# A hybrid decoder trunk on one core: one plain gate/up pair fewer in three FFNs, with the fourth of the seven products ahead of the third and the weights rounded four items ahead

## The chip, the core and the metric

The kernel runs on one core of one Trainium2 chip. The engines have short names in the profile: PE is TensorE (matmuls; PEld is its weight load), DVE is VectorE, ACT is ScalarE, POOL is GpSimd and SP is SyncE, which here only issues DMAs. Each engine takes its instructions in its own fixed order, and they wait for each other by semaphores. The metric is the device time of one execution in microseconds; of several runs the median counts.

## The reference

Two layers, each with an FFN, a mixer (a gated linear recurrence and a sliding-window attention side by side) and a second FFN, every one between two RMSNorms. Sequence 512, model width 1024, hidden width 2816 (22 tiles of 128), all float32. The change lies in the FFNs:

```python
def swiglu(h, w_gate, w_up, w_down):
    return (jax.nn.silu(h @ w_gate) * (h @ w_up)) @ w_down

for l in range(DEPTH):
    h = rms_norm(x, gn[0])
    x = x + 0.5 * rms_norm(swiglu(h, w_ffn1_gate[l], w_ffn1_up[l], w_ffn1_down[l]), gn[1])
    ...
    h = rms_norm(x, gn[4])
    x = x + 0.5 * rms_norm(swiglu(h, w_ffn2_gate[l], w_ffn2_up[l], w_ffn2_down[l]), gn[5])
```

## The kernel before

**Matmuls in float32 by three passes.** Each operand is split into a high half, rounded to a format that TensorE takes at full speed, and a low half, the remainder. A product is hi x hi + hi x lo + lo x hi, three matmuls (`mm3`, line 381). For weights the halves are called `whi` and `wlo`; `wlo` is first used by the third matmul of a group. Rounding is done while the kernel runs: ScalarE casts (L325), and the remainder comes either from VectorE (a subtraction, L332) or, for some items, from a negation on ScalarE (L329) and a DMA of GpSimd's queue that adds the raw weight onto it (L330).

**The stream of weights.** `Stream` (line 156) holds the order in which the weights are used as a list of items, each one tile of 128 x 1024 or less. Raw tiles (`w32`, four buffers) are loaded by SP's DMAs (L241, L244); rounded ones have six buffers (`WS`). `ahead` (line 342) rounds items until `most` = `AHEAD` = 3 items past the current one are done, as long as fewer than six are in use.

**An FFN's first half** is 22 pairs of a gate tile and an up tile, `gated(...)` or `fast(...)`. In the first FFN of layer 0 the first seven pairs are plain; in the other three FFNs the first `PLAIN` = 4 are: two in one opening group (`quad`), the others one by one, each two products `project` of 8 x 3 matmuls of 512 columns. During them VectorE and ScalarE prepare sums of the activations (`pre.sums()`, L564, L459 to L466, L401, L402): four are needed, two are issued after the opening group and one ahead of each single pair.

**The other pairs are fast blocks** (`sevenths`, line 851): gate and up together are a 2 x 2 block product done with seven products instead of eight, each 4 x 3 matmuls of 256 columns. A block uses four weight items: a (products 1 and 2; negation and DMA), b (5 and 7; the sums L312 and L313 are rounded, remainder by VectorE), c (6 and 4; sums L318 and L319, remainder by VectorE) and d (product 3; half a tile, negation and DMA). VectorE puts the products together in L875, L877, L882 and L883, ScalarE copies the first product (L865) and applies the silu in place (L895), and VectorE multiplies (L896). While block k runs, the weights of later blocks are rounded.

**The second half** is the down product (`down`, line 637), which starts with four plain weight items and goes on with a seven-product scheme of its own over rows, whose items are quarters (`quarter`, line 255; casts L282, remainders L287). Its first operands are the first four results of the FFN, split by L401 (ScalarE) and L402 (VectorE); the last fast block issues that split after its second product (`early`, line 887).

**What sets the order.** TensorE's order is that of the program text (with some coroutines put in by a clock of the planner's own). The other engines' instructions are ordered by the framework's scheduler; those marked `pin` keep the text's order among themselves. So the text's order on TensorE is exact, and on VectorE, ScalarE and the DMA queues a small edit can move instructions.

Of the kernel before, what the change touches and what calls it, by code (L numbers as in the profile page):

```python
# [33 lines left out]
    head=2600.0, level=5000.0, last=3400.0, chunks=2600.0, blocks=350.0, norm=2370.0, gate=8000.0,  # L34
    values=1200.0, scores=2000.0, exp=9000.0, shares=4500.0, turn=1900.0, turned=3000.0, rest=1200.0, lent=4200.0, apart=4000.0, block=2000.0, pair=4000.0, att0=1260.0, att1=12300.0,
)
W32, WS, AHEAD, TAIL, PLAIN, FIRST, EARLY, LATE = 4, 6, 3, 4, 4, 7, 4, 8
TURN = 0
LEAD = 8
ORDER = ("p1", "p6", "p2", "p7", "p5", "p4", "p3")  # L40
# [5 lines left out]
def trunk(ctx: ExitStack, tc: tile.TileContext, xin, wall, gains, lbT, hgain, sinks, c_dist, c_mask, c_ident, out):  # L46
# [12 lines left out]
    def nm(s):  # L59
        seq[0] += 1  # L60
        return f"{s}_{seq[0]}"

    def big(dt=F32, shape=None):
        return sb.tile(shape or [P, S], dt, tag="s", name=nm("s"), bufs=SLOTS)
# [4 lines left out]
    def acc():  # L69
        return ps.tile([P, S], F32, tag="acc", name=nm("acc"), bufs=5)  # L70

    def aux():
        return ps.tile([P, S], F32, tag="aux", name=nm("aux"), bufs=3)
# [82 lines left out]
    class Stream:  # L156
# [27 lines left out]
        def gates(self):  # L184
# [6 lines left out]
            self.plain(1)  # L191

        def rows(self, kt, fast):


# [183 lines left out]
    ws = Stream()  # L379
# [7 lines left out]
    def wmm(o, b, mv, start, stop, poll=True):  # L387

        mm3(o, b[2:], mv, start, stop)
        ws.used(b)  # L390
        if poll:
            order.poll()
# [217 lines left out]
    class Late(Quarters):  # L610
# [23 lines left out]
        def raw(self, half, i):  # L634
            return [cut(self.src[self.k0 + 4 + k], HALF[half]) for k in range(4)] if i else self.x1

    def down(src, kt, l, n, nxt, fast):


# [176 lines left out]
    def quad(pre, halves):  # L816

        o = [acc() for _ in range(4)]
        blocks = {}
        ws.pinned = halves  # L820
        for half in (0, 1) if halves else (None,):
            c = WHOLE if half is None else HALF[half]
            for k in range(KT):
                order.until(lambda: pre.have[half or 0] > k)
                for j in range(4):
                    if (k, j) not in blocks:
                        blocks[k, j] = ws.next(uses=2 if halves else 1)
                    wmm(o[j][:, c], blocks[k, j], cut(pre.h[k], c), k == 0, k == KT - 1)
            ws.pinned = False
        return o  # L830

    def project(pre, get=acc):
        o = get()
        for k in range(KT):
            wmm(o, ws.next(), pre.h[k], k == 0, k == KT - 1)
        return o
# [12 lines left out]
    H2 = S // 2  # L849

    def sevenths(pre, between=lambda: None):

        def product(o, it, c, n):
            x = pre.operand(n)
            for k in range(4):
                wmm(o, ws.block(it, c + k), x[k], k == 0, k == 3)

        p1, p26, p57, p43 = acc()[:, :H2], acc(), acc(), aux()  # L860
        s, v = big()[:, :H2], big(F32, [P, 2, H2])
        m = sb.tile([P, 4, H2], F32, tag="m", name=nm("m"), bufs=1)
        w = ws.whole()
        product(p1, w, 0, 1)
        nc.scalar.copy(s, p1)  # L865
        product(p26[:, :H2], w, 4, 2)
        between()
        w = ws.whole()
        product(p57[:, :H2], w, 0, 5)
        product(p57[:, H2:], w, 4, 7)  # L870
        c = ws.whole()
        product(p26[:, H2:], c, 0, 6)
        pairs = [p.rearrange("p (i t) -> p i t", i=2) for p in (p26, p57, p43)]

        nc.vector.tensor_tensor(m[:, 0:4:2, :], pairs[0], s.unsqueeze(1).to_broadcast([P, 2, H2]), op=ALU.add)  # L875

        nc.vector.tensor_tensor(v, pairs[1], m[:, 2:3, :].to_broadcast([P, 2, H2]), op=ALU.add)  # L877
        w = ws.whole()
        product(p43[:, H2:], w, 4, 3)
        product(p43[:, :H2], c, 4, 4)  # L880

        nc.vector.tensor_tensor(m[:, 3, :], p57[:, :H2], v[:, 1, :], op=ALU.add)  # L882
        nc.vector.tensor_tensor(m[:, 1:3, :], pairs[2], v[:, ::-1, :], op=ALU.add)  # L883
        return m

    def fast(pre, a, start):
        def early():
            if j == FT - 1:
                for i in range(EARLY):
                    a[i] = split(a[i])  # L890

        for j in range(start, FT):
            m = sevenths(pre, early)
            z = big(F32, [P, 2, H2])
            nc.scalar.activation(out=m[:, 0:2, :], in_=m[:, 0:2, :], func=AF.Silu)  # L895
            nc.vector.scalar_tensor_tensor(z, m[:, 0:2, :], -1.0, m[:, 2:4, :], op0=ALU.mult, op1=ALU.mult)  # L896
            a.append(z.rearrange("p i t -> p (i t)"))

    def ffn(l, n, pre, nxt, halves=True):
        a = []  # L900

        def gated(og, ou):
            z, u = big(), big()
            if first:
                pin(nc.vector.tensor_tensor(z, og, pre.rb, op=ALU.mult))
                nc.scalar.activation(out=z, in_=z, func=AF.Silu)
                nc.vector.tensor_tensor(u, ou, pre.rb, op=ALU.mult)
                nc.vector.tensor_tensor(u, u, z, op=ALU.mult)
            else:
                nc.scalar.activation(out=z, in_=og, func=AF.Silu)  # L910
                pin(nc.vector.tensor_tensor(u, ou, z, op=ALU.mult))
            a.append(u)

        first = isinstance(pre, First)
        o = quad(pre, halves)
        if first:
            o.append(project(pre))
            o.append(project(pre, aux))
            order.until(lambda: pre.rb is not None)
        if not first:  # L920
            pre.sums()
            pre.sums()
        for j in range(2):
            gated(o[2 * j], o[2 * j + 1])
        if first:
            gated(o[4], o[5])
            for j in range(3, FIRST):
                if j > 3:
                    order.until(lambda: pre.laid)
                    pre.sums()  # L930
                if j == 4:
                    pre.sums()
                gated(project(pre), project(pre))
            fast(pre, a, FIRST)
        else:
            for j in range(2, PLAIN):
                pre.sums()
                gated(project(pre), project(pre))
            fast(pre, a, PLAIN)
        return down(a, FT, l, n + 1, nxt, True)  # L940
# [129 lines left out]
    def mixer(l, pre, nxt):  # L1070
# [177 lines left out]
        def branches(get):  # L1248

            v = sevenths(pre)  # L1250
            src = get()
            for i in range(2):
                g = big(F32, [P, 2, H2])
                nc.scalar.activation(out=g, in_=v[:, 2 * i : 2 * i + 2, :], func=AF.Tanh, scale=-0.5 if i else 0.5)
                p = acc()
                for k in range(4):
                    wmm(p, ws.next(), src[k], k == 0, k == 3)
                g = g.rearrange("p i t -> p (i t)")
                nc.vector.scalar_tensor_tensor(g, g, 1.0, p, op0=ALU.add, op1=ALU.mult)
                yield g  # L1260
# [36 lines left out]
    pre = First()  # L1297
# [69 lines left out]
    for l in range(DEPTH):  # L1367
        pre = ffn(l, 0, pre, (l, 2), halves=l > 0)
        pre = mixer(l, pre, (l, 4))
        pre = ffn(l, 4, pre, (l + 1, 0) if l + 1 < DEPTH else None)  # L1370
# [81 lines left out]
```

## Time and profile before

| | us |
|---|---|
| three runs | 2100.14, 2100.54, 2103.34 |
| median | 2100.54 |
| the profiled execution | 2100.66 |
| its span, first to last instruction | 2098.9 |

The profile is of one execution. Its page gives each engine's busy time; the chain of waits goes back from the last instruction to what released each step; the timeline lists instructions with their start, their length and, in brackets, the idle time of the engine before them and what ended it. A row marked x2 stands for two instructions in a row. Starts of two neighbouring rows are the better measure of pace, since the lengths overlap a little. TensorE's granted clock is 0.999 of full speed over the span.

| engine | busy, us | share of the span |
|---|---|---|
| TensorE, matmuls | 2090.3 | 100% |
| VectorE | 1550.5 | 74% |
| ScalarE | 1122.4 | 53% |
| GpSimd | 154.2 | 7% |

### The profile page before, as it was taken

What the parts mean: (1) busy time and instruction counts of PE and PEld (TensorE: products, weight loads), DVE (VectorE), ACT (ScalarE), POOL (GpSimd) and SP (SyncE); (2) the same over time, 40 slices, a digit from 0 to 9 for tenths busy, and PEclk for the clock granted to TensorE, in tenths of its full rate; (3) what the DMA queues carried; (4) which work ended last, traced back from release to release, by engine and by line L of the source; (5) the groups of instructions that cost most, each with busy time, mean ns of one, the idle gap of its engine ahead of it and who ended that gap; (6) DMA issues with size and microseconds to landing.
All of it is one profiled execution on the core that took longest, in us unless ns stands there. A gap on an engine that the chain in (4) does not pass through costs nothing.

```text
span 2098.9 us, 35207 instructions
## 1 busy us (share of the span) xinstructions
PE 2090.3 (100%) x13549; PEld 1875.3 (89%) x13549; DVE 1550.5 (74%) x2705; ACT 1122.4 (53%) x1899; POOL 154.2 (7%) x188
## 2 busy tenths in 40 slices
PE   9999999999999999999999999999999999999998
PEld 8899988887888999998899998898778989999987
DVE  5877886766776777789587778767687758777884
ACT  6555564456454555556455556554653545555562
POOL 0011000000000011110001110000000000111000
PEclk9999999999999999999999999999999999999999
DMA  8577653312236357774447775632122563677651
GB/s 246 152 181 184 178 157 135 111 61 71 71 101 203 127 122 182 181 198 122 154 114 176 183 181 150 191 120 92 51 81 61 136 193 103 159 182 181 184 160 51
DMA packets 148071, 298.35 MB, mean 142 GB/s; under 512 B 16992, under 2 KB 74816, under 8 KB 147904
## 3 DMA queue, kind: packets, MB, share of 16 engines
q1 hardware_dynamic: 122416, 228.16, 33.2%
q0 software_dynamic: 25344, 67.91, 18.7%
q8 instruction: 106, 1.74, 0.3%
q14 instruction: 61, 0.50, 0.1%
q10 hardware_dynamic: 144, 0.05, 0.0%
HBM read 213.43 MB, written 14.73 MB: 109 GB/s over the span
## 4 chain that ended last, share of the span: by engine, by line
PE 88%; DMA 0%; DVE 0%; ACT 0%; SPq 0%; issue 0%; ACTq 0%
PE acc L115 64%; PE aux L115 22%; PE aux L125 1%; PE acc L125 1%; DMA wlo<-w 0%; DMA w<-wall 0%; SPq L241 0%; DVE s L402 0%; ACT whi L282 0%; DVE s L731 0%; ACT s L600 0%; DVE s L712 0%; DVE s L896 0%; DVE wlo L287 0%; ACT m L895 0%
## 5 line engine op out<-in xcount | busy, mean ns | idle before, releaser
L115 PE MATMUL acc<-s,whi 128*128 128x256 f32 (+1 forms) x4952 | 1059.3, 311 | 0.4 <-ACT whi L325 0.3
L115 PEld LDWEIGHTS acc<-s,whi 128*128 128x128 f32 x4952 | 808.0, 191 | 51.3 <-issue 3.2
L115 PE MATMUL acc<-s,wlo 128*128 128x256 f32 (+1 forms) x2476 | 766.6, 310 | 0.1
L115 PEld LDWEIGHTS acc<-s,wlo 128*128 128x128 f32 x2476 | 472.6, 191 | 25.0 <-DVE wlo L332 0.4
L325 ACT CAST whi<-w 128x1024 fp32r<-128x1024 f32 (+1 forms) x341 | 316.6, 948 | 237.6 <-PE acc L115 95.5
L115 PE MATMUL acc<-whi,s 128*128 128x512 f32 x1264 | 413.6, 393 | 0.1
L325 ACT CAST whi<-tt 128x1024 fp32r<-128x1024 f32 x154 | 161.4, 1048 | 326.5 <-DVE tt L319 184.2
L332 DVE TENSOR_TENSOR wlo<-w,whi 128x1024 fp32r<-128x1024 f32 (+1 forms) x181 | 218.3, 1215 | 151.4 <-ACT whi L325 149.6
L115 PEld LDWEIGHTS acc<-whi,s 128*128 128x128 f32 x1264 | 237.1, 188 | 54.7 <-ACT whi L325 1.6
L332 DVE TENSOR_TENSOR wlo<-tt,whi 128x1024 fp32r<-128x1024 f32 x154 | 188.1, 1221 | 98.8 <-ACT whi L325 98.7
L115 PE MATMUL acc<-wlo,s 128*128 128x512 f32 x632 | 246.4, 390 | 0.0
L115 PE MATMUL aux<-s,whi 128*128 128x256 f32 (+1 forms) x1248 | 230.4, 285 | 0.0
L330 POOL DMA_DIRECT2D wlo<-w x160 | 137.8, 863 | 1258.6 <-ACT wlo L329 704.9
L115 PE MATMUL aux<-whi,s 128*128 128x512 f32 x592 | 196.7, 390 | 0.0
L115 PEld LDWEIGHTS aux<-s,whi 128*128 128x128 f32 x1248 | 195.2, 192 | 1.1 <-issue 0.5
L115 PE MATMUL aux<-s,wlo 128*128 128x256 f32 (+1 forms) x624 | 177.5, 284 | 0.0
L115 PEld LDWEIGHTS acc<-wlo,s 128*128 128x128 f32 x632 | 118.7, 188 | 23.4
L115 PEld LDWEIGHTS aux<-whi,s 128*128 128x128 f32 x592 | 111.1, 188 | 22.8
L329 ACT ACTIVATE wlo<-w 128x1024 fp32r<-128x1024 f32 (+1 forms) x160 | 129.8, 844 | 0.0
L401 ACT CAST s<-s 128x512 fp32r<-128x512 f32 (+1 forms) x164 | 88.4, 580 | 71.5 <-DVE s L460 67.9
L115 PEld LDWEIGHTS aux<-s,wlo 128*128 128x128 f32 x624 | 119.8, 192 | 0.3
L115 PE MATMUL aux<-wlo,s 128*128 128x512 f32 x296 | 115.2, 389 | 0.0
(186 smaller groups left out, 2128.6 us busy)
## 6 DMA issues: line engine op xcount, KB each, us to landing
w<-wall SPq DMA_DIRECT2D x267, 512.0 KB, 3.7
wlo<-w POOLq DMA_DIRECT2D x83, 512.0 KB, 5.5
w<-wall SPq DMA_DIRECT2D x288, 128.0 KB, 3.3
wlo<-w POOLq DMA_DIRECT2D x77, 256.0 KB, 3.3
x_d<-s SPq DMA_DIRECT2D x48, 256.0 KB, 2.1
s<-x_d SPq DMA_DIRECT2D x48, 256.0 KB, 5.5
w<-wall SPq DMA_DIRECT2D x34, 256.0 KB, 3.0
s<-wall SPq DMA_DIRECT2D x64, 128.0 KB, 3.6
```

The source lines that it names most:

```text
L115: nc.tensor.matmul(o, lhsT, rhs, start=start, stop=stop)
L125: nc.tensor.transpose(o, src, ident)
L325: i = nc.scalar.copy(it.hi[:, c], w[:, c])
L329: nc.scalar.mul(it.lo[:, c], w[:, c], -1.0)
L330: nc.gpsimd.dma_start(it.lo[:, c].bitcast(F32), w[:, c], accum_op=ALU.add)
L332: nc.vector.tensor_tensor(it.lo[:, c], w[:, c], it.hi[:, c].bitcast(F32), op=ALU.subtract)
L401: nc.scalar.copy(hi, src)
```

## The change

Three edits. `PLAIN` goes from 4 to 3: in three of the four FFNs one pair that was plain becomes a fast block, and the two sums that were issued one each ahead of two single pairs are both issued ahead of the one that is left. Inside a fast block, and in the mixer's gate blocks, which call the same function, product 4 is issued ahead of product 3, so item c is used up before d is taken. And while an FFN's fast blocks run, `most` is 4 instead of 3. Line numbers after 877 shift: what was L882 and L883 is L881 and L882, L895 and L896 keep theirs.

```diff
-W32, WS, AHEAD, TAIL, PLAIN, FIRST, EARLY, LATE = 4, 6, 3, 4, 4, 7, 4, 8
+W32, WS, AHEAD, TAIL, PLAIN, FIRST, EARLY, LATE = 4, 6, 3, 4, 3, 7, 4, 8
...
-        w = ws.whole()
-        product(p43[:, H2:], w, 4, 3)
         product(p43[:, :H2], c, 4, 4)
+        product(p43[:, H2:], ws.whole(), 4, 3)
...
+        ws.most = AHEAD + 1
         for j in range(start, FT):
             m = sevenths(pre, early)
...
+        ws.most = AHEAD
...
             for j in range(2, PLAIN):
-                pre.sums()
+                for _ in range(2 // (PLAIN - 2)):
+                    pre.sums()
                 gated(project(pre), project(pre))
```

The scheduler answers with other orders on VectorE and ScalarE. The first place is one lap of VectorE in the fast blocks of the second FFN, before the change (`tt` are the summed weights: L312 and L313 make b's, L318 and L319 c's; `m` is the block's result):

```order
L312 TENSOR_TENSOR tt_8716<-w_1524_8517,w_1525_8519 128x512
L313 TENSOR_TENSOR tt_8716<-w_1525_8519 128x512
L332 TENSOR_TENSOR wlo_8715<-tt_8716,whi_8714 128x1024
L318 TENSOR_TENSOR tt_8747<-tt_8716,w_1525_8519 128x512
L319 TENSOR_TENSOR tt_8747<-tt_8747,w_1524_8517 128x512
L875 TENSOR_TENSOR m_8680<-acc_8675,s_8678 128x2x256
L877 TENSOR_TENSOR s_8679<-acc_8676,m_8680 128x512
L332 TENSOR_TENSOR wlo_8746<-tt_8747,whi_8745 128x1024
L882 TENSOR_TENSOR m_8680<-acc_8676,s_8679 128x256
L883 TENSOR_TENSOR m_8680<-aux_8677,s_8679 128x512
L896 TENSOR_SCALAR s_8798<-m_8680 128x512
```

The same lap after the change:

```order
L875 TENSOR_TENSOR m_8619<-acc_8614,s_8617 128x2x256
L877 TENSOR_TENSOR s_8618<-acc_8615,m_8619 128x512
L332 TENSOR_TENSOR wlo_8624<-tt_8625,whi_8623 128x1024
L318 TENSOR_TENSOR tt_8657<-tt_8625,w_1515_8439 128x512
L881 TENSOR_TENSOR m_8619<-acc_8615,s_8618 128x256
L319 TENSOR_TENSOR tt_8657<-tt_8657,w_1514_8437 128x512
L882 TENSOR_TENSOR m_8619<-aux_8616,s_8618 128x512
L332 TENSOR_TENSOR wlo_8656<-tt_8657,whi_8655 128x1024
L896 TENSOR_SCALAR s_8737<-m_8619 128x512
L312 TENSOR_TENSOR tt_8752<-w_1534_8564,w_1535_8566 128x512
L313 TENSOR_TENSOR tt_8752<-w_1535_8566 128x512
```

b's remainder and c's sums, which stood ahead of L875, now stand behind L877, and c's remainder behind L882. ScalarE's order in that lap is the copy, the casts of b and c, then the rounding of d and of the next a, then the silu, before and after; of d and a it takes the two casts first before the change, and d's cast and negation first after it. The lap of the first FFN keeps the old order on both engines.

The second place is ScalarE at the end of the fast blocks of the second FFN, before the change (L895 is the silu of the last block but one, L865 the copy of the last block's first product, L325 the cast of a plain item of the down product, L282 casts of its quarters, L401 those of its first operands):

```order
L895 ACTIVATE m_9956<-m_9956 128x512
L865 COPY s_10087<-acc_10083 128x256
L401 COPY s_10124<-s_7733 128x512
L325 COPY whi_10200<-w_1764_10047 128x1024
L401 COPY s_10128<-s_7737 128x512
L401 COPY s_10132<-s_7821 128x512
L325 COPY whi_10223<-w_1765_10052 128x1024
L401 COPY s_10136<-s_7909 128x512
L282 COPY whi_10281<-w_1776_10097 128x512 x2
L282 COPY whi_10332<-w_1787_10147 128x512 x2
```

After the change:

```order
L895 ACTIVATE m_10022<-m_10022 128x512
L325 COPY whi_10163<-w_1755_9966 128x1024
L325 COPY whi_10237<-w_1774_10094 128x1024
L325 COPY whi_10270<-w_1775_10099 128x1024
L282 COPY whi_10305<-w_1778_10134 128x512 x2
L282 COPY whi_10393<-w_1789_10167 128x512 x2
L865 COPY s_10157<-acc_10153 128x256
L401 COPY s_10218<-s_7733 128x512
L401 COPY s_10222<-s_7737 128x512
```

The copy and the first operands' casts, which stood ahead of the quarters, now stand behind all four of their casts. VectorE's remainders follow in the same way (L287, L875, L402), and the first FFN ends in the same new order.

## The prediction, on record before the changed kernel ran

> **What bounds the kernel now.** I read the page first, then the chain of waits, and only then the timelines of VectorE and ScalarE inside one fast block.
>
> ```profile
> span 2098.9 us, 35207 instructions
> PE 2090.3 (100%) x13549; PEld 1875.3 (89%) x13549; DVE 1550.5 (74%) x2705; ACT 1122.4 (53%) x1899; POOL 154.2 (7%) x188
> ```
> ```profile
> 717.69 43.37 PE acc L115 x276
> 761.06 2.88 PE aux L115 x24
> ```
>
> TensorE is busy for the whole span. The chain gives its pace: 24 matmuls of 256 columns, the two last products of a fast block, take 2.88 us, 0.120 each; a block has 84, 10.08 us. The 276 matmuls from 717.69 are 120 of the opening group of the FFN, two plain pairs of 48 and the first 60 of a block; 43.37 - 180 x 0.120 leaves 21.77 for the two pairs, 10.88 each. So the kernel is bound by TensorE, and something else decides whether it stays so: how late the rounded weights come. Here is one fast block on VectorE, late in the second FFN (start, length, instruction, idle time before it and what ended it), and then ScalarE's rows around it.
>
> ```profile
> 903.64 0.68 DVE L875 TENSOR_TENSOR m<-acc,s 128x512 f32<-128x512 f32 x1
> 904.36 0.69 DVE L877 TENSOR_TENSOR s<-acc,m 128x512 f32<-128x512 f32 x1
> 904.97 1.22 DVE L332 TENSOR_TENSOR wlo<-tt,whi 128x1024 fp32r<-128x1024 f32 x1
> 906.10 0.42 DVE L882 TENSOR_TENSOR m<-acc,s 128x256 f32<-128x256 f32 x1
> 906.43 0.68 DVE L883 TENSOR_TENSOR m<-aux,s 128x512 f32<-128x512 f32 x1
> 908.36 0.69 DVE L896 SCALAR_TENSOR_TENSOR s<-m 128x512 f32<-128x512 f32 x1 [1.25 <-ACT m L895]
> 908.97 0.68 DVE L312 TENSOR_TENSOR tt<-w,w 128x512 f32<-128x512 f32 x1
> 909.57 0.68 DVE L313 TENSOR_TENSOR tt<-w 128x512 f32<-128x512 f32 x1
> 911.37 1.22 DVE L332 TENSOR_TENSOR wlo<-tt,whi 128x1024 fp32r<-128x1024 f32 x1 [1.11 <-ACT whi L325]
> 912.51 0.68 DVE L318 TENSOR_TENSOR tt<-tt,w 128x512 f32<-128x512 f32 x1
> 913.23 0.69 DVE L319 TENSOR_TENSOR tt<-tt,w 128x512 f32<-128x512 f32 x1
> 913.84 0.68 DVE L875 TENSOR_TENSOR m<-acc,s 128x512 f32<-128x512 f32 x1
> ```
> ```profile
> 907.72 0.62 ACT L895 ACTIVATE m<-m 128x512 f32<-128x512 f32 x1
> 910.29 1.05 ACT L325 CAST whi<-tt 128x1024 fp32r<-128x1024 f32 x1 [1.70 <-DVE tt L313]
> 914.01 1.05 ACT L325 CAST whi<-tt 128x1024 fp32r<-128x1024 f32 x1 [2.67 <-DVE tt L319]
> 914.97 1.56 ACT L325 CAST whi<-w 128x512 fp32r<-128x512 f32 x2
> 917.91 0.62 ACT L895 ACTIVATE m<-m 128x512 f32<-128x512 f32 x1
> ```
>
> VectorE repeats after 913.84 - 903.64 = 10.20 us, longer than TensorE's 10.08, and no wait in that lap is for TensorE. It is a ring through both engines. From one silu (L895) to the next: product L896 0.64, L312 0.61, L313 0.60, cast of item b 0.72, its remainder (L332) 1.08, L318 1.14, L319 0.72, cast of c 0.78, first cast after it 0.96, then the two casts and two negations of d and the next a 2.94 up to the silu: 10.19. The busy shares (74%, 53%) hide this. TensorE loses nothing because 18 laps of 0.12 us eat only 2 us of the lead.
>
> **The change, part by part.** *Fewer plain pairs.* Three times 10.88 becomes 10.08: -2.4 us, all on TensorE's path.
>
> *The ring in these three FFNs.* By the order of the changed program, VectorE now takes b's remainder and L318, L319 after L875 and L877; c's cast waits for L319, and the silu still stands behind d's and a's rounding on ScalarE. The new lap, by the same rows: silu to L896 0.64, to L312 0.61, to L313 0.60, to L875 0.60 (as L312 to L313), to L877 0.72, to b's remainder 0.61, to L318 1.14, to the next independent one 0.60, to L319 0.33 (as L882 to L883), to c's cast 0.78, 0.96, then 2.94: 10.53 us. That is 0.45 over TensorE's 10.08, with no TensorE wait in it. Is there a lead to pay from? The last of a lap's results is the low half of the a-weights for the block after next:
>
> ```profile
> 771.99 0.61 ACT L325 CAST whi<-w 128x512 fp32r<-128x512 f32 x1
> 772.51 0.63 ACT L329 ACTIVATE wlo<-w 128x512 fp32r<-128x512 f32 x1
> 773.98 1.05 ACT L329 ACTIVATE wlo<-w 128x1024 fp32r<-128x1024 f32 x1
> ```
> ```profile
> 775.33 0.86 POOL L330 DMA_DIRECT2D wlo<-w  x1 [1.03 <-ACT wlo L329]
> ```
> ```profile
> wlo<-w POOLq DMA_DIRECT2D x83, 512.0 KB, 5.5
> wlo<-w POOLq DMA_DIRECT2D x77, 256.0 KB, 3.3
> ```
>
> L875 to c's cast is 4.18 (0.72 to 0.78 in that lap), then 0.96 + 2.94 to the silu; a's negation ends 0.1 later, POOL's DMA starts 0.30 after it (775.03 to 775.33) and lands 5.5 later: 14.0 us after L875. L875 can run 7.2 us into a block (60 matmuls), and the block after next needs that half at its third matmul, 20.16 + 0.24 - 7.2 = 13.2 us after L875. So the lead is already 0.8 short, and the ring's 0.45 goes to TensorE in every block.
>
> The first blocks. VectorE prepares four sums ahead of the fast blocks:
>
> ```profile
> 735.30 1.28 DVE L564 TENSOR_TENSOR s<-s,s 128x512 f32<-128x512 f32 x2
> 739.61 0.68 DVE L312 TENSOR_TENSOR tt<-w,w 128x512 f32<-128x512 f32 x1
> ```
>
> One sum takes 4.31 us here. Before, a whole plain pair hid the last; now the first block starts at 743.0 instead of 753.9 (761.06 less 60 x 0.120, and less 10.88). If the third sum still starts at 735.3, the fourth ends at 743.9; L318, L319 and c's cast follow at 745.4, a's negation ends 2.94 + 0.96 + 0.1 later at 749.4 and its DMA lands at 755.2. It is due at 743.0 + 10.08 + 0.24 = 753.3: 1.9 us of stall. So an FFN loses 1.9 at its second block, 0.8 at the fourth, then 15 x 0.45 = 6.8: 9.5, and three FFNs 28.5. Bounds: a landing 1 us shorter saves the 0.8 and 1.0 of the 1.9 (23 in all); one half a microsecond longer makes the way over the DMA (two blocks in 8.5 + 6.0 - 0.24 + 7.2 = 21.5) slower than the ring, 0.65 a block (36).
>
> *The end of the fast blocks, in all four FFNs.* With four items ahead, ScalarE has the rounding of the first quarter items (L282, four casts) ahead of the copy L865 of the last block and ahead of the L401 casts that make the first operands of the down product; before, the four L401 stood ahead of L282. This is how it goes now in the first FFN:
>
> ```profile
> 233.56 4.57 DMA wlo<-w
> ...
> 244.72 0.63 ACT whi L282
> ...
> 245.37 0.69 DVE wlo L287
> ```
> ```profile
> 240.94 0.40 PE L115 MATMUL acc<-whi,s 128*128 128x512 f32 x1
> ```
>
> The raw quarters land late, since one of their buffers waits for the last d accumulation (233.56 to 238.13); the last L282 starts at 244.72, 3.8 us after the down product has begun at 240.94. In the new order L865 follows at +0.52, L401 at +0.78, and on VectorE L287 at 245.37, L875 0.6 later and the low half (L402, 0.69) 0.6 after that: 247.3. TensorE needs it at its third matmul, 240.94 + 0.45. Stall 5.9 us. In the other three FFNs the last d comes with the longer ring:
>
> ```profile
> 927.55 0.86 POOL L330 DMA_DIRECT2D wlo<-w  x1 [8.39 <-DVE m L883]
> ```
> ```profile
> 938.40 0.62 ACT L282 CAST whi<-w 128x512 fp32r<-128x512 f32 x1 [0.59 <-DMA w<-wall]
> ```
>
> The last L282 starts 10.85 after that DMA. Now d's DMA starts 4.18 + 0.96 + 1.15 + 0.30 = 6.6 after L875, so the last L282 starts 17.4 after it and the low half is there at 20.0, while the down product is due 13.2 after L875 and at its third matmul 13.6. Stall 6.4; three FFNs 19.2. Bounds: if the quarters came early, L282 would still wait for the buffers of the last block, freed at its end: two casts, L865, L401 and L402 are then 2.7 us each (11 in all); the extra transfer that now stands ahead of the quarters in SP's queue makes 7 each (28).
>
> *TensorE's clock.* Five to six idle microseconds are new to it. The end of the program shows what thin use does (stretch, busy times, then the granted clock):
>
> ```profile
> 2088.00:2090.00 2.00, 2.00 (x15) 1.79 (x13) 0.69 (x1) 0.59 (x1) 0.00 (x0) 1.00 0.00 0
> 2090.00:2092.00 2.00, 0.38 (x2) 0.00 (x0) 1.38 (x2) 0.82 (x3) 0.00 (x0) 1.00 0.81 251
> 2094.00:2096.00 2.00, 0.86 (x4) 0.45 (x4) 0.62 (x1) 0.59 (x1) 0.00 (x0) 0.56 0.19 60
> ```
>
> Dense work ends at 2090, and a mean of 0.56 over 2094 to 2096 is half speed from about 2094.2 on. I take it that each of the four stalls does this and that the way back is as long: 4.2 us at half speed lose 2.1, four times 8.4. No row shows the way back; the bounds are nothing, and the first 24 matmuls of the down product at half speed, 5.4 each (22). [...]
>
> *Product four ahead of three.* Both end the block together; TensorE's count and L883's wait stay. It gives d 12 matmuls, 1.44 us, more. In the first block d's accumulation starts at about 747.8 (c's cast 745.4, then 0.96 + 1.15 + 0.30) and lands 3.3 later at 751.1; its first use of the low half is now due at 743.0 + 8.64 + 0.24 = 751.9, in the old place at 750.4, which would have been a stall of 0.7. In later blocks it has more than 1 us to spare. So I cost it at nothing. In the gate blocks of the mixer the order of VectorE and ScalarE is unchanged: nothing. In the first FFN the lap is the old one, 10.20: nothing.
>
> **The sum.** -2.4 + 28.5 + 5.9 + 19.2 + 8.4 = +59.6. The profiled execution took 2100.66 us (span 2098.9 and 1.8 around it), 0.1 over the median of 2100.54; so 2100.7 + 59.6 = 2160.3.
>
> **The rivals.** (1) The clock does not fall, as the two matmuls that can run in each stall may be enough: 2152. For it: in 2090 to 2092 it still stood at 1.00 with 0.38 us of work. (2) The quarters land in time, so that the ends cost 2.7 each, with the clock kept: 2100.7 - 2.4 + 28.5 + 11 = 2138. Against it: in the first FFN their chain of waits is the old one. (3) Faster: the lead is longer than I count and eats the ring as it does now. An FFN drifts 19 x 0.45 = 8.6 us; if the a-weights landed a block earlier than worked out (10 us), and the first down operands were rounded before the quarters are due, only the saved work is left: 2098.3. It decides from a lead of 8.6 us on; the rows give -0.8. (4) The fourth item changes nothing: six rounded buffers might cap it at the old depth. Then the old lap of 10.20 stays and the time is within 0.2% of before; the order speaks against it.
>
> **How the numbers follow.** Forecast 0.47, rival 1 0.27, rival 2 0.13, still slower (landings of 6 us and a longer return) 0.05, rival 3 0.05, rival 4 0.03. About 0.2%, 4.2 us, is what a measurement of this kernel can tell. Faster 0.05, same 0.03, slower 0.92. The range takes in rival 2 with a cheaper ring (2130) and, upward, landings of 6 us with the sum (2160.3 + 7.5) or a dearer return (2160.3 + 13.6, the bound): 2130 to 2175.
>
> **What would show it.** Right: L875 to L875 about 10.5 us in three FFNs and 10.2 in the first; TensorE waiting on the accumulation DMA at the first product of most blocks; four gaps of 5 to 7 us at the start of the down products, ended by L402, with the clock at half after them. Wrong: laps of 10.1 to 10.2 there, TensorE without gaps at the down products, or a clock of 1.00 throughout.

## The result, and the profile after

| | before | after |
|---|---|---|
| median of four runs, us | 2100.91 | 2169.58 |
| lowest to highest | 2100.14 to 2103.34 | 2167.07 to 2171.31 |
| the profiled execution | 2100.66 | 2167.94 |
| its span | 2098.9 | 2165.8 |

The ratio of the times is 1.0324, with a 95% interval of 1.0306 to 1.0342. The prediction was 2160.3, with a range of 2130 to 2175.

The page of the changed kernel, first part, and TensorE's waits, largest first (total, times, longest):

```profile
span 2165.8 us, 35664 instructions
PE 2108.6 (97%) x13657; PEld 1887.4 (87%) x13657; DVE 1561.9 (72%) x2729; ACT 1131.6 (52%) x1914; POOL 159.4 (7%) x194
```
```profile
PE acc L115 <- DMA wlo<-w: 25.1, 32, 2.4
PE acc L115 <- ACT s L401: 22.2, 4, 6.0
PE acc L125 <- DVE s L731: 2.9, 1, 2.9
```

TensorE was busy for all of the span and is now idle for 57 us of it. Two waits are new: 32 for the accumulation that makes `wlo`, and four for L401, the high half of a first down operand. VectorE and ScalarE have hardly more work than before (1550.5 and 1122.4 us then), so it is not work that was added.

One lap of VectorE in the second FFN, to be read beside the lap shown before; behind it ScalarE's silu that its L896 waits for:

```profile
864.77 0.69 DVE L875 TENSOR_TENSOR m<-acc,s 128x512 f32<-128x512 f32 x1 [0.44 <-issue]
865.49 0.69 DVE L877 TENSOR_TENSOR s<-acc,m 128x512 f32<-128x512 f32 x1
866.10 1.21 DVE L332 TENSOR_TENSOR wlo<-tt,whi 128x1024 fp32r<-128x1024 f32 x1
867.24 0.68 DVE L318 TENSOR_TENSOR tt<-tt,w 128x512 f32<-128x512 f32 x1
867.84 0.42 DVE L881 TENSOR_TENSOR m<-acc,s 128x256 f32<-128x256 f32 x1
868.17 0.68 DVE L319 TENSOR_TENSOR tt<-tt,w 128x512 f32<-128x512 f32 x1
868.77 0.68 DVE L882 TENSOR_TENSOR m<-aux,s 128x512 f32<-128x512 f32 x1
870.02 1.22 DVE L332 TENSOR_TENSOR wlo<-tt,whi 128x1024 fp32r<-128x1024 f32 x1 [0.57 <-ACT whi L325]
873.49 0.69 DVE L896 SCALAR_TENSOR_TENSOR s<-m 128x512 f32<-128x512 f32 x1 [2.25 <-ACT m L895]
...
875.30 0.68 DVE L875 TENSOR_TENSOR m<-acc,s 128x512 f32<-128x512 f32 x1
```
```profile
872.84 0.61 ACT L895 ACTIVATE m<-m 128x512 f32<-128x512 f32 x1
```

From L875 to L875 it is 875.30 - 864.77 = 10.53 us. VectorE waits 2.25 us for the silu, which waits for d's and a's rounding, which waits for L319; no row in the lap waits for TensorE. Most laps of the three FFNs measure 10.52 to 10.56. Some are longer. The next one but one is the longest in the loops, 13.98, and here is why (GpSimd's DMA for an a-item, its size and the time from issue to landing, then TensorE):

```profile
883.75 0.86 POOL L330 DMA_DIRECT2D wlo<-w  x1 [1.03 <-ACT wlo L329]
```
```profile
wlo<-w POOLq DMA_DIRECT2D x1, 512.0 KB, 6.9
```
```profile
890.73 0.38 PE L115 MATMUL acc<-s,wlo 128*128 128x256 f32 x1 [1.82 <-DMA wlo<-w]
```

883.75 + 6.9 = 890.65: the landing releases the matmul. Its neighbours land in 5.2 to 5.3 us, and TensorE waits 0.9 us or less for them.

The end of the fast blocks in the first FFN, rows of the engines in the order of their start:

```profile
244.31 0.62 ACT L282 CAST whi<-w 128x512 fp32r<-128x512 f32 x1 [1.12 <-DMA w<-wall]
244.83 0.36 ACT L865 COPY s<-acc 128x256 f32<-128x256 f32 x1
...
245.09 2.18 ACT L401 CAST s<-s 128x512 fp32r<-128x512 f32 x4
245.56 0.68 DVE L875 TENSOR_TENSOR m<-acc,s 128x512 f32<-128x512 f32 x1
245.77 0.80 PE L115 MATMUL acc<-whi,s 128*128 128x512 f32 x1 [4.88 <-ACT s L401]
246.17 1.89 DVE L402 TENSOR_TENSOR s<-s,s 128x512 fp32r<-128x512 f32 x3
```

The last cast of a quarter waits for its load, and the copy and the casts of the first down operands stand behind it; TensorE stands still for 4.88 us. Then the clock, in stretches of 2 us (busy times of the engines; the third number from the end is the granted clock):

```profile
240.00:242.00 2.00, 0.88 (x8) 0.68 (x6) 1.73 (x2) 0.74 (x2) 0.00 (x0) 1.00 0.92 261
242.00:244.00 2.00, 0.00 (x0) 0.00 (x0) 1.39 (x2) 1.11 (x2) 0.00 (x0) 0.75 0.73 229
244.00:246.00 2.00, 0.23 (x1) 0.23 (x2) 1.04 (x2) 1.69 (x4) 0.00 (x0) 0.50 0.86 238
246.00:248.00 2.00, 2.00 (x5) 1.17 (x6) 2.00 (x5) 1.27 (x3) 0.00 (x0) 0.50 0.98 275
248.00:250.00 2.00, 2.00 (x7) 1.57 (x6) 1.97 (x5) 0.00 (x0) 0.00 (x0) 0.55 0.91 251
250.00:252.00 2.00, 2.00 (x11) 1.65 (x10) 1.24 (x3) 0.93 (x2) 0.00 (x0) 1.00 0.87 271
```

It falls to half about 2 us into the gap (the gap begins at 240.9, and a mean of 0.75 over 242 to 244 is half speed from 243 on), and TensorE, busy again, does 5 and 7 matmuls in stretches of 2 us; in the last one, at full speed, it does 11.

**Where the 66.9 us of span went.** Matching events of the two traces stand apart by 6.5 us behind the first FFN's end, by 28.6 in the second FFN's down product, 49.7 and 66.9 behind the third and fourth. Split into loops and ends, summed as the next section says, this gives:

| term | predicted | measured |
|---|---|---|
| work saved | -2.4 | -2.4 (not seen apart) |
| loops of three FFNs | 28.5 | 13.9 + 12.7 + 10.4 = 37.0 |
| gaps at the four ends | 25.1 | 5.05 + 6.12 + 6.01 + 5.66 = 22.8 |
| half speed after them | 8.4 | 2.1 + 2.9 + 2.8 + 1.9 = 9.7 (all that an end loses behind its gap) |
| sum | 59.6 | 67.1 |

### The profile page after: what moved, and what is told of

It is laid out like the page before. It is cut to its first block, busy times and chain, and to the rows that moved or that the text cites. A ratio compares the mean times of both kernels' runs of the same rounds, so it can differ in the third digit from the quotient of the medians.

```text
span 2165.8 us, 35664 instructions
## 1 busy us (share of the span) xinstructions
PE 2108.6 (97%) x13657; PEld 1887.4 (87%) x13657; DVE 1561.9 (72%) x2729; ACT 1131.6 (52%) x1914; POOL 159.4 (7%) x194
## 3 DMA queue, kind: packets, MB, share of 16 engines
q8 instruction: 107, 1.75, 0.3%
## 4 chain that ended last, share of the span: by engine, by line
PE 69%; issue 26%; DMA 2%; DVE 1%; ACT 1%; SPq 1%; POOL 1%; POOLq 0%; ACTq 0%; DVEq 0%
PE acc L115 51%; PE aux L115 16%; PE aux L125 1%; DMA wlo<-w 1%; DMA w<-wall 1%; SPq L241 1%; PE acc L125 1%; POOL wlo L330 1%; DVE wlo L332 0%; ACT whi L325 0%; DMA s<-xin 0%; DVE tt L319 0%; DVE m L875 0%; ACT whi L282 0%; DVE tt L318 0%
## 5 line engine op out<-in xcount | busy, mean ns | idle before, releaser
L115 PE MATMUL acc<-s,wlo 128*128 128x256 f32 (+1 forms) x2488 | 769.7, 309 | 25.7 <-DMA wlo<-w 25.1
L325 ACT CAST whi<-w 128x1024 fp32r<-128x1024 f32 (+1 forms) x341 | 318.9, 942 | 246.6 <-PE acc L115 93.9
L115 PE MATMUL acc<-whi,s 128*128 128x512 f32 x1264 | 420.4, 399 | 22.2 <-ACT s L401 22.2
L325 ACT CAST whi<-tt 128x1024 fp32r<-128x1024 f32 x160 | 167.7, 1048 | 373.0 <-DVE tt L319 245.0
L332 DVE TENSOR_TENSOR wlo<-w,whi 128x1024 fp32r<-128x1024 f32 (+1 forms) x175 | 211.8, 1216 | 168.8 <-ACT whi L325 140.1
L332 DVE TENSOR_TENSOR wlo<-tt,whi 128x1024 fp32r<-128x1024 f32 x160 | 195.3, 1221 | 65.1 <-ACT whi L325 65.1
L115 PE MATMUL aux<-s,whi 128*128 128x256 f32 (+1 forms) x1296 | 239.2, 285 | 0.0
L330 POOL DMA_DIRECT2D wlo<-w x166 | 142.9, 863 | 1295.5 <-DVE wlo L332 485.3
L115 PEld LDWEIGHTS aux<-s,whi 128*128 128x128 f32 x1296 | 202.7, 192 | 1.1 <-issue 0.5
L115 PE MATMUL aux<-s,wlo 128*128 128x256 f32 (+1 forms) x648 | 184.3, 284 | 0.1
L896 DVE SCALAR_TENSOR_TENSOR s<-m 128x512 f32<-128x512 f32 x72 | 49.8, 692 | 133.5 <-ACT m L895 133.5
L329 ACT ACTIVATE wlo<-w 128x1024 fp32r<-128x1024 f32 (+1 forms) x166 | 139.3, 847 | 0.0
L115 PEld LDWEIGHTS aux<-whi,s 128*128 128x128 f32 x592 | 111.1, 188 | 22.8
L401 ACT CAST s<-s 128x512 fp32r<-128x512 f32 (+1 forms) x164 | 87.6, 580 | 77.7 <-DVE s L460 75.2
```

What stands on the lines that cost most here:

```text
L115: nc.tensor.matmul(o, lhsT, rhs, start=start, stop=stop)
L325: i = nc.scalar.copy(it.hi[:, c], w[:, c])
L329: nc.scalar.mul(it.lo[:, c], w[:, c], -1.0)
L330: nc.gpsimd.dma_start(it.lo[:, c].bitcast(F32), w[:, c], accum_op=ALU.add)
L332: nc.vector.tensor_tensor(it.lo[:, c], w[:, c], it.hi[:, c].bitcast(F32), op=ALU.subtract)
L401: nc.scalar.copy(hi, src)
```

## The experiments

Two sums are made in the same way for every trace. "Loops" is, for the three FFNs that the change shortens, every lap from L875 to L875 but the last one of an FFN, less 10.08 each; it is negative where VectorE begins behind and catches up. "Ends" is where the 41st matmul of the down product starts, less where it would start without a pause behind the last fast block (40 x 0.227), summed over four FFNs. The kernel before ran beside every group, at 2100.5 to 2101.1.

| run | median, us | ratio, 95% interval | loops, us | ends, us |
|---|---|---|---|---|
| before | 2100.91 | | 2.8 | 0.0 |
| after | 2169.58 | 1.0324, 1.0306 to 1.0342 | 36.9 | 32.5 |
| e1_most | 2128.71 | 1.0132, 1.0117 to 1.0147 | 3.0 | 27.2 |
| e2_plain | 2126.91 | 1.0124, 1.0109 to 1.0139 | 27.9 | 0.0 |
| e3_swap | 2100.76 | 1.0002, 0.9992 to 1.0011 | 3.2 | 0.0 |
| e4_plain_most | 2164.12 | 1.0302, 1.0287 to 1.0317 | 31.5 | 31.3 |
| e5_after_again | 2167.17 | 1.0320, 1.0305 to 1.0336 | 35.5 | 32.2 |
| e6_dummy | 2162.50 | 1.0299, 1.0284 to 1.0315 | 41.7 | 27.1 |
| e7_end | 2135.62 | 1.0166, 1.0149 to 1.0183 | 33.9 | 0.0 |
| e8_silu_first | 2127.31 | 1.0133, 1.0103 to 1.0162 | 23.1 | 0.0 |
| e9_old_lap | 2106.83 | 1.0028, 1.0018 to 1.0039 | 7.0 | 0.0 |
| e10_old_lap_silu | 2107.04 | 1.0029, 1.0018 to 1.0041 | -0.4 | 0.0 |
| e11_dummy_short | 2166.71 | 1.0313, 1.0298 to 1.0328 | 35.7 | 29.7 |
| e12_fourth_sum_later | 2104.33 | 1.0019, 1.0010 to 1.0028 | -2.1 | 0.0 |

### One edit at a time

The fourth rounded item alone:

```diff
+        ws.most = AHEAD + 1
         for j in range(start, FT):
...
+        ws.most = AHEAD
```

> The kernel before with the fourth rounded item as its only edit. My theory: two separate costs. The order of the lap stays the old one, so VectorE's lap stays 10.20 us and the loops lose nothing; the ends of all four FFNs get the new order (quarters' casts ahead of the copy and of the first operands), so each costs a stall of 5 to 7 us and 2 to 3 us of clock: 4 x 8 = 32, about 2133 us. Rival A, the fourth item lengthens the loops too: 2165 or more with laps of 10.5. Rival B, the fourth item is harmless without the missing plain pair: 2101.

Measured 2128.71, +28.0, some 4 us less than I expected. The laps are 10.20 as before and the four ends cost 27.2, so nearly all of it is the ends. Rivals A and B fall.

One plain pair fewer alone:

```diff
-W32, WS, AHEAD, TAIL, PLAIN, FIRST, EARLY, LATE = 4, 6, 3, 4, 4, 7, 4, 8
+W32, WS, AHEAD, TAIL, PLAIN, FIRST, EARLY, LATE = 4, 6, 3, 4, 3, 7, 4, 8
...
-                pre.sums()
+                for _ in range(2 // (PLAIN - 2)):
+                    pre.sums()
```

> The kernel before with one plain pair fewer in three FFNs as its only edit (the two sums ahead of the last plain pair, three items ahead as before). My theory: the ends stay in the old order and lose nothing; the saved work is -2.4; the lap has a period of three blocks, in which one lap has the silu ahead of the a-weights' rounding, by the rows 8.9 + 10.8 + 10.8 = 30.5 us for three against TensorE's 30.24, so the loops lose 1 to 2 us each after a stall of about 2 at the second block: 3 x 3.5 - 2.4 = +8, about 2109 us. Rival A, the late sums are guilty for the whole loop: 2130 to 2140 with laps of 10.5. Rival B, the saved work is all that is left: 2098.5.

Measured 2126.91, +26.2: my number missed by 18 us. The ends cost nothing, as expected, but the loops cost 27.9. Three laps take 11.21 + 10.68 + 9.71 = 31.6 us, a mean of 10.53, and I had expected 30.5:

```profile
856.37 0.68 DVE L875 TENSOR_TENSOR m<-acc,s 128x512 f32<-128x512 f32 x1
867.05 0.68 DVE L875 TENSOR_TENSOR m<-acc,s 128x512 f32<-128x512 f32 x1
876.76 0.69 DVE L875 TENSOR_TENSOR m<-acc,s 128x512 f32<-128x512 f32 x1 [1.88 <-ACT whi L325]
```
```profile
859.37 0.38 PE L115 MATMUL acc<-s,wlo 128*128 128x256 f32 x1 [1.11 <-DMA wlo<-w]
890.97 0.38 PE L115 MATMUL acc<-s,wlo 128*128 128x256 f32 x1 [1.11 <-DMA wlo<-w]
```

I had averaged a short lap (the one with the silu ahead of a's rounding) with two long ones. That is wrong twice. TensorE cannot use a lap that is shorter than its own 10.08, and the short lap is bought with a later a-item, for which TensorE then waits 1.1 us in one block of three (the two gaps are 31.6 apart). Rival A, the loop is what the missing pair costs, stands, and its time came close; but the laps are not the 10.5 each that it expected. VectorE's order here is a third one, with L875 between L318 and L319 in two laps of three, and not the lap of the changed kernel.

The product order alone:

```diff
-        w = ws.whole()
-        product(p43[:, H2:], w, 4, 3)
         product(p43[:, :H2], c, 4, 4)
+        product(p43[:, H2:], ws.whole(), 4, 3)
```

> The kernel before with the fourth product ahead of the third as its only edit. The order of every engine but TensorE is the one before. My theory: no change, 2101 us within 2. Rival, c's weights, used 1.44 us earlier, come late: some tenths of a microsecond in each of 69 fast blocks, 2110 to 2130, with TensorE waiting on VectorE's remainder (L332) in the fourth product.

Measured 2100.76, ratio 1.0002: nothing, as expected.

The other two edits together, with the product order left as it was:

> The changed kernel with the products back in their old order, three ahead of four; VectorE, ScalarE and the queues keep the changed order. My theory: d's half item is due 1.44 us earlier and has that to spare, except in the first blocks, where three stalls of at most 0.7 come: 2169.6 to 2172. Rival, the swap is what pushes the lap over TensorE's block: below 2150.

Measured 2164.12. It lies between the two expectations, nearer to mine, but below it: the product order is not what costs most, and yet this kernel is 3.0 and 5.5 us under the two measurements of the full change. Since the two edits alone give 26.2 + 28.0 = 54.2 and together 63.4, 9.2 us come only when they meet: the ends grow by 4.1 and the loops by 3.6; the remaining 1.5 I did not place. For the ends the prediction has a reason (the last d-item is later where the lap is longer, and a quarter's load waits for d's buffer); no run tests it apart.

### The full change once more

Nothing is edited.

> The changed kernel once more, on the chip of the next three, as their yardstick. Theory that the product order costs nothing: 2164 to 2170, and the 5.5 us by which it stood over the kernel with the old product order come from single late landings, elsewhere than in the first trace. Rival, the order itself costs: again 2169 or more, with the long laps in the same blocks.

Measured 2167.17, inside the theory's range and under the rival's 2169. Of the rival's two signs one came: the long laps stand in the same blocks (11.40, 10.98 and 12.23 where the first trace has 11.81, 11.05 and 13.98). That sign is weak. The first of the three is as long with the old product order (11.95 in e4), and in e6 and e11 below, which have the new order, the other two are 10.52 to 10.87. The loops are 35.5 here against 31.5 with the old product order, and 33.9 to 41.7 in all five traces with the new one. The intervals of the ratios overlap (1.0305 to 1.0336 and 1.0287 to 1.0317). So whether the product order costs some 3 us in this company is open; alone it costs nothing. This trace has its longest lap, 13.99, elsewhere, behind the stall of a second block:

```profile
1126.05 0.39 PE L115 MATMUL acc<-s,wlo 128*128 128x256 f32 x1 [2.21 <-DMA wlo<-w]
```
```profile
1124.00:1126.00 2.00, 0.00 (x0) 0.00 (x0) 1.52 (x3) 0.69 (x1) 0.00 (x0) 1.00 0.94 186
1126.00:1128.00 2.00, 1.95 (x12) 1.95 (x13) 1.23 (x1) 2.00 (x4) 0.29 (x1) 0.75 0.72 225
1128.00:1130.00 2.00, 2.00 (x12) 2.00 (x11) 0.14 (x1) 2.00 (x4) 0.97 (x2) 0.50 0.96 278
1130.00:1132.00 2.00, 2.00 (x17) 2.00 (x17) 1.75 (x3) 0.24 (x2) 0.46 (x1) 0.90 0.79 144
```

A gap of 2.21 us inside the loop was enough to halve the clock for 3.4 us.

### The clock in the gap

24 useless matmuls are put where TensorE stands still:

```diff
         ws.most = AHEAD
+        p = aux()
+        for _ in range(24):
+            nc.tensor.matmul(p[:, :P], ones, ones, start=True, stop=True)
```

> The changed kernel with 24 matmuls of float32 ones (128x128) into a free bank behind each FFN's last fast block, about 5.2 us of useless work put into the stall of 5 to 6. Theory that the clock falls in the stall and is paid for afterwards: the first operands come as late as before, TensorE keeps 1.00, and the 2.1 to 3.1 us that the first 18 down matmuls lost four times come back: 2157 to 2161. Rival, those matmuls are slow for another reason (operands or weights that trickle in): no change, or slower by what the useless work adds.

Measured 2162.50, 4.7 below the full change that ran beside it, where 6 to 10 were expected. Useless work made the kernel faster, but only by half. The trace is that of the slowest of its runs (2168.33; its loops cost 41.7, so the ends are compared alone). The clock kept 1.00:

```profile
246.00:248.00 2.00, 1.60 (x11) 1.05 (x9) 1.93 (x4) 2.00 (x6) 0.00 (x0) 1.00 0.74 231
248.00:250.00 2.00, 1.99 (x9) 1.63 (x10) 2.00 (x4) 0.38 (x1) 0.00 (x0) 1.00 0.87 270
```

and the ends cost 27.1 instead of 32.2. Of these, 23.9 are the pause up to the first down matmul, 22.7 in the run beside it: at the first two ends the filling took 5.45 and 5.28 us and ran past the operand by some 0.1 us at most, at the other two it ended 1.2 and 0.9 us ahead of it. So the pause is 1.2 longer because the operands came later, not because of the filling; why they did was not taken apart. What stays apart from the pause fell from 9.6 to 3.2 us. The 3.2 are 0.8 an end with the clock at 1.00, of which 0.4 is a wait for the first low half (L402). So the rival is right in a small part, and the fall itself costs about 6.4 us over the four ends.

With 17 of them:

> The changed kernel with 17 instead of 24 of the useless matmuls behind each FFN's last fast block: 17 x 0.23 = 3.9 us, which ends 1 us or more before the first operand comes. Theory that half speed after the stall costs 2.1 to 3 us an end, and that the longer filling gave half of that back by running past the operand: now the ends cost the gap alone, 5 to 6.7 us each, 23 in all against 32, so 2167.2 - 9 = 2158. Rival, the 1 to 2 us of gap that stay are enough for the clock to fall: 2164 to 2168.

Measured 2166.71: the rival's number. At the first end the 17 took 3.96 us, 0.23 for one of 128 columns in plain float32, where the rounded ones of 512 columns start every 0.227. The remaining idle time was 1.41 and 1.75 us at the first two ends, and the clock stayed; it was 2.46 and 1.97 at the other two, and the clock fell. The ends cost 6.2 + 6.5 + 8.6 + 8.4 = 29.7. Behind its pause an end loses 0.8 us where the clock stayed and 2.2 and 2.4 where it fell, so a fall costs some 1.5 us here. How much filling it takes was mis-sized by me. That the longer filling had given gain back by running past the operand, as I assumed, is not so: it ran past by some 0.1 us at most.

### The order at the end

```diff
         for j in range(start, FT):
+            if j == FT - 1:
+                ws.most = AHEAD
             m = sevenths(pre, early)
```

> The changed kernel with the look-ahead back at three items for the last fast block of each FFN, so that ScalarE casts the first down operands (L401) ahead of the quarters (L282). My theory: the four ends cost under 1 us each and the loops stay as they are: 2170 - 32 = 2138, within 4. Rival, the quarters are what is late and the wait only moves on to them: 2150 or more, with a gap of 4 to 6 us some 20 us later.

Measured 2135.62, 31.6 below the full change beside it. ScalarE now casts the first operands ahead of the quarters, in the second FFN:

```profile
941.74 0.62 ACT L401 CAST s<-s 128x512 fp32r<-128x512 f32 x1
942.26 1.05 ACT L325 CAST whi<-w 128x1024 fp32r<-128x1024 f32 x1
943.21 1.13 ACT L401 CAST s<-s 128x512 fp32r<-128x512 f32 x2
...
947.74 2.05 ACT L282 CAST whi<-w 128x512 fp32r<-128x512 f32 x3 [0.93 <-DMA w<-wall]
```

No pause is left at any end, and none came later. The quarters were never needed early; their place in the queue was the whole cost.

### The ring in the loop

ScalarE is held to the silu ahead of the next a-item's cast and negation, with three items ahead:

```diff
-            nc.scalar.activation(out=m[:, 0:2, :], in_=m[:, 0:2, :], func=AF.Silu)
+            pin(nc.scalar.activation(out=m[:, 0:2, :], in_=m[:, 0:2, :], func=AF.Silu))
...
-                if u < 3 or self.pinned:
+                if u < 3 or self.pinned or (it.kind == "a" and self.silu):
                     pin(i)
```

> One plain pair fewer and the product order as in the changed kernel, three items ahead, and ScalarE held to the silu ahead of the next a-weights' cast and negation in every fast block (both were behind each other the other way round). Theory of the ring: the silu no longer waits for a's 2 us, a lap of both engines falls from 10.5 to about 8.5, below TensorE's 10.08; what is left is the stall at each second block (1.7 as in the run with only the plain pair taken away): 2100.7 - 2.4 + 5.1 = 2103.5, between 2101 and 2107, laps of 10.1. Rival, the way of the a-weights over the DMA sets the pace and not the ring: 2115 or more with TensorE waiting on it in most blocks.

Measured 2127.31, with runs from 2123 to 2137: the rival's number, though both theories were half right. The ring is gone: most laps are 10.08, TensorE's own. But a's DMA now starts only behind the silu and has no room, so single landings cost whole microseconds:

```profile
781.57 0.86 POOL L333 DMA_DIRECT2D wlo<-w  x1 [2.56 <-ACT s L868]
```
```profile
wlo<-w POOLq DMA_DIRECT2D x1, 512.0 KB, 8.0
```
```profile
789.58 0.39 PE L115 MATMUL acc<-s,wlo 128*128 128x256 f32 x1 [2.07 <-DMA wlo<-w]
```

781.57 + 8.0 is 789.57. So a lap has two ways that must both be shorter than 10.08: the ring, and the way of the a-weights over the DMA. Here the second one decides.

Next, VectorE is held to the old lap instead: L875 goes behind the sums of c (L318, L319), and ScalarE is left alone.

```diff
+    def behind(i, j):
+        if j is not None:
+            tc.add_manual_dep(i.ins, j.ins.name, ...)
+        return i
...
-        nc.vector.tensor_tensor(m[:, 0:4:2, :], pairs[0], ...)
+        i = nc.vector.tensor_tensor(m[:, 0:4:2, :], pairs[0], ...)
+        if ws.fast:
+            behind(i, ws.g)
```

> One plain pair fewer and the product order as in the changed kernel, three items ahead, and VectorE held to the sums of item c (L318, L319) ahead of L875 in every fast block, as in the kernel before; nothing is fixed on ScalarE. Theory that the order of the lap is what the missing plain pair costs: laps of 10.2, a-weights with 3 us to spare, the stall of 1.7 at each second block and no lead for the 0.12 us of each lap, 3 x (1.7 + 2.0) - 2.4 = +8.7, about 2109.5 us. Rival, the late sums cost it whatever the order: 2122 or more, with laps of 10.5 on average.

Measured 2106.83, 20 us below the kernel that has the same plain pairs and the scheduler's lap. The laps are 10.20 (L881 is L875 of this kernel):

```profile
844.05 0.68 DVE L881 TENSOR_TENSOR m<-acc,s 128x512 f32<-128x512 f32 x1
854.25 0.68 DVE L881 TENSOR_TENSOR m<-acc,s 128x512 f32<-128x512 f32 x1
```

The order of the lap, not the lateness of the sums, is what the missing pair cost for the most part; the product order, which differs too, costs nothing alone. The second blocks still stall, 0.8, 2.2 and 1.4 us.

With the negation of a also behind the silu:

```diff
-                    nc.scalar.mul(it.lo[:, c], w[:, c], -1.0)
+                    i = nc.scalar.mul(it.lo[:, c], w[:, c], -1.0)
+                    if it.kind == "a":
+                        behind(i, self.silu)
```

> The kernel of the run with VectorE held to the old lap, and on ScalarE the negation of the a-weights also held behind the silu, its cast left free (so only 0.96 us and not 2 are taken out of the way of the silu, and the a-weights come 1 us earlier than in the run with the silu ahead of both). Theory: the ring falls to 9.2, TensorE sets 10.08 everywhere, the a-weights keep 2 us to spare, so only the second blocks stall: 2100.7 - 2.4 + 3 x 1.7 = 2103.5, within 3. Rival, the a-weights' landing still has no room: single laps of 11 to 12 as in that run, 2110 or more.

Measured 2107.04: between the two. The laps are 10.08 and the loops sum to -0.4, yet the time did not improve on the run before: the second blocks stall as they did, and one lap of 11.45 came from an a-item without room.

Last, the fourth sum is issued behind the plain pair:

```diff
-                for _ in range(2 // (PLAIN - 2)):
-                    pre.sums()
+                pre.sums()
                 gated(project(pre), project(pre))
+            pre.sums()
```

> The kernel of the run before (old lap on VectorE, a's negation behind the silu), and the fourth sum of the activations issued behind the last plain pair instead of ahead of it, so that VectorE takes the sums of the first block's item c ahead of it and the a-weights of the second block are rounded some 4 us earlier. Theory: that is all that the stall of 1.5 to 2.2 us at each second block is made of; TensorE's waits for the accumulation fall from 5.5 us to under 1, and 2107.0 becomes 2101 to 2102.5, level with before within 0.2%, as 2.4 us of work saved is all there is to gain. Rival, the stall comes from the fourth sum's own use or from the landing: no change, 2106 or more.

Measured 2104.33. The stall of the second block is gone. In its place TensorE waits 0.3 to 0.6 us for the fourth sum itself, and four landings later in the loops cost 0.4 to 1.2 (total, times, longest):

```profile
PE acc L115 <- DMA wlo<-w: 2.8, 4, 1.2
PE acc L115 <- DVE s L410: 1.0, 3, 0.3
PE acc L115 <- ACT s L409: 0.6, 1, 0.6
```

It misses my number by 2 us, and is slower than the kernel before by 0.10% to 0.28%. No version that I tried beats the kernel before.

## Why the prediction was right, and where it was off

**The bound.** TensorE's pace of 10.08 and the ring of 10.20 behind it were read rightly: where a kernel keeps the old order (e1, e3), nearly all laps are 10.19 to 10.21.

**The new lap.** Worked out as 10.53 from the old trace's rows, and 10.53 in the new one. That the order makes it, and not the work, is shown by e2 against e9 for the missing plain pair: with the scheduler's order the loops cost 27.9, with the old one 7.0. The regular lap of 10.53 needs the fourth item as well: e2 without it has laps of 11.2, 10.7 and 9.7, and no run shows why its mean is 10.53 too.

**The loops: the term that was mis-sized**, 28.5 against 37.0. The ring was right, but the a-weights' way over the DMA is almost as long. In the lap behind the one shown the DMA starts 883.75 - 875.30 = 8.45 us after L875; with a landing of 5.3, less 0.24, plus the 7.2 up to the second next L875, that is 20.7 for two laps against the ring's 21.06. What a landing takes over 5.6 us is therefore paid in full. In the second FFN three take 5.8, 5.9 and 6.9, in the third two 5.9 and 6.4; three times, once in each FFN, GpSimd issued the DMA 0.7 us later than usual behind the negation, which I did not explain. I had a landing half a microsecond longer as a bound (36), and took the median landing for all in the sum. A fall of the clock inside the loop, which I had not thought of, adds 1.7.

**The second blocks.** 1.9 us of stall each, worked out; 0.9, 2.4 and 1.4 in the trace. The 0.8 worked out for the fourth block is 0.6, 1.8 and 0.7 there, the middle one behind the landing of 6.4. The mechanism (c's sums behind the fourth sum) is shown by e12, where moving that sum takes the stall away.

**The ends.** Stalls of 5.9 and three times 6.4 were worked out; measured are gaps of 5.0 to 6.1, in the places named and for the reason named (e1, e7). One detail was wrong: TensorE stands still for L401 at the first matmul, not for L402 at the third; behind that wait the low half is another 0.4 us late (e6). And the 13.2 us to the start of the down product should have been 12.96 (two blocks less 7.2), which would make each of the three stalls 6.6.

**The clock.** 8.4 against 9.7 at the ends. Rival 1, that it stays, is refuted by the stretches above. The prediction took 4.2 us of work at half speed behind each stall; it was 4.1, 5.8, 5.4 and 3.5. That most of the slowness behind the gap is the clock, and not the operands, is shown by e6: with the clock kept, 3.2 of some 9.6 us stay. So the fall itself costs about 6.4, less than the 8.4.

**The rest.** Rival 2 priced the ends at 2.7 if the quarters came in time; they did not. Rival 3, a longer lead, and rival 4, a fourth item without effect, are excluded by e2 and e1. The product order at nothing is right alone and open by some 3 us with the others.

## What to carry to other kernels

Where a scheduler orders two engines, count the lap of the ring through both before and after an edit, row by row; 0.3 us more in a lap that had 0.12 too much already cost over ten times the work that was saved. More look-ahead was not free here (28 us, e1): in ScalarE's one order what is prepared early stands ahead of what is needed now, so look-ahead should end before the stage does. A transfer whose median just fits was paid by its slow landings (5.2 to 5.3 us for most in the changed kernel's loops, 5.8 to 6.9 for the slow ones); take the slow tail, not the median, for the lead.

## What the hardware showed that was not expected

**The half-speed pieces of one trace lie on a grid.** In the trace of the full change, ahead of the program's end, they are 3.41 or 6.83 us long, and they start at 242.99, 891.52, 959.79, 1325.01 and 2034.99 us: 190, 210, 317 and 525 times 3.413 us after the first one. Gaps of 1.82 us there and of 2.21 in e5 halved the clock, and so did the 1.97 and 2.46 left over in e11, while the 1.41 and 1.75 left over in e11 and gaps of 1.78 and even 2.42 us in the third FFN of the first trace left it at 1.00. The grid may explain a part of that: it cuts the gap of 2.42 us into 0.79 and 1.63. But the gaps of 1.82 and 1.78 lie each within one step, and half speed followed the first alone. What decides is not shown. Here a gap of some 2 us cost 1.7 us more in one place and nothing in another.

**The accumulating DMA has a wide tail.** In the fast blocks of the three FFNs, 512 KB took 5.2 to 5.3 us in most cases, but 6.9 once in the trace of the full change and 6.9 to 8.0 in four blocks in a row in e8, and 256 KB, mostly 3.3, up to 5.8 in e2. What else was under way in those stretches was not taken apart.
